# The one-tile up group of the second half of the MLP is worked between the two down groups of the first half

## The chip, the cores and the metric

The kernel runs on one NeuronCore of one Trainium2 chip. The metric is the device time of one execution in microseconds (us). Three executions of the kernel before took 1300.86, 1300.80 and 1301.01 us, a median of 1300.86.

## The reference, cut to what matters

One layer: a gated token mixer, then a convolutional gated MLP, then a last RMSNorm. Only the MLP is touched. There are 256 tokens, a width of 2048 and an inner width of 5504, which is 43 tiles of 128 features.

```
def conv_ffn(x, g_norm, w_up, conv_k, conv_b, w_down):
    h = rms_norm(x, g_norm)
    up = h @ w_up                                   # 2048 -> 2 * 5504: a gate and a value
    t = up.shape[1]
    pad = jnp.pad(up, ((0, 0), (1, 1), (0, 0)))
    up = (pad[:, :t] * conv_k[0] + pad[:, 1:t + 1] * conv_k[1]
          + pad[:, 2:t + 2] * conv_k[2] + conv_b)   # width 3 over the tokens
    gate, val = jnp.split(up, 2, axis=-1)
    return x + (jax.nn.silu(gate) * val) @ w_down   # 5504 -> 2048
```

All of it is float32.

## The kernel before

**Split numbers.** A float32 product is made of three products of float32r operands. Each weight piece is loaded into a raw slot (SP queue, L272), ScalarE writes its rounded high part (`high`, L316), and VectorE writes the low part, piece minus high part (`low`, L319). TensorE multiplies high by high, low by high and high by low (L483 to L485, or L459 and L467 where the weights are the stationary operand).

**Pieces and slots.** All weights lie in one stream of pieces, in the order in which `weight_stream` lists the groups. A usual piece is 512 KB (1024 columns by 128 rows, or two row tiles of 512 columns). There are five raw slots (`RAW`), each free again when high and low of its piece are made, and the load of the piece five places later waits for that. Six unit slots hold a high and a low part; a unit is free when TensorE has used it. At piece i the program prepares pieces up to i + 4 (`AHEAD`), then runs the small tasks that earlier steps have left for i, then issues TensorE's products. Each engine works its own list in order and waits on semaphores for the others.

**The MLP in two parts.** `FF_BLOCKS` cuts the 43 tiles into 22 and 21. Of each part the up groups come first, two feature tiles each (8 pieces of 512 KB, 4 PSUM banks); the second part has an odd number of tiles, so its first group, ("up", 22), has a single tile: 8 pieces of 256 KB and 2 banks. Behind an up group stand its evictions: `combine` (L854, L856) adds the two halves of the banks, `conv` (L1225 to L1233) scales and convolves, `gate` (L1238, L1240) makes silu(gate) times value, `split` (L1147, L1148) makes high and low of the result for the down groups. Then come two down groups, ("down", n, 0) and ("down", n, 1), for the left and the right 1024 output columns, one piece of 512 KB per feature tile.

**Pairs with seven products.** In a down group some pairs of pieces are worked with seven products where the plain way has eight (`FF_SEVEN`). For such a pair VectorE makes a half low and a full low (`plain`), then sums the two raw pieces in place (`summed`: L396, L400, L401; or L398 to L401 where the two raw slots don't adjoin), then makes two more full lows of the sums (`summed` and `last`). Only after these are the pair's two raw slots free. The second group of the first part has five such pairs, at its pieces 2, 6, 10, 14 and 18. `LATE_SUMS` names a pair whose sums are queued one step later. Some low parts are made early, stored in HBM and read back by the POOL queue (L350) in place of the subtraction: in this group those of pieces 1, 5 and 9.

**Banks.** A down group holds four banks for its plain products, and one each for the products 1, 5, 7 and 6 of its pairs: all eight. Behind the last pair `combine` of `wide_step` empties the extra four: `one` (L586, L591, L592) frees the banks of 1, 6 and 7, the first instruction of `both` (L586, on two rows) frees that of 5. At the end of the group two additions of 1024 columns (L1286) empty the other four. The next group takes the pairs of banks that were freed first.

Below, d0 to d21 are the pieces of ("down", 0, 1), u0 to u7 those of ("up", 22), and n0 to n7 those of ("up", 23), the first two-tile up group of the second part.

Of the kernel before, what the change touches and what calls it, by code (L numbers as in the profile page):

```python
# [18 lines left out]
KD = D // 128  # L19
# [4 lines left out]
DFF = 5504  # L24
# [17 lines left out]
RAW = 5  # L42
TB = 2
SUMS_LATE = 1
LATE_SUMS = ((("down", 0, 1), 2), (("down", 1, 1), 1))
ODD_AMONG = 1
UNITS = (4, 2)
WAKE = 20
# [22 lines left out]
def weight_stream():  # L71

    groups, order = {}, []

    def add(key, kind, w, pieces):
        groups[key] = (kind, w, pieces)
        order.extend([key] * len(pieces))

    def by_two(row0, nk, *blocks):
        return [([row0 + k for k in range(k0, min(k0 + 2, nk))], blocks) for k0 in range(0, nk, 2)]

    def nat(key, w, row0, nk, c0):
        add(key, "nat", w, by_two(row0, nk, (c0, 512)))

    def qk(j):
        add(("qk", j), "ws", "w_in", by_two(0, KD, (Q0 + j * 256, 256), (K0 + j * 256, 256)))

    def wide(key, w, c0, tiles):
        add(key, "wide", w, [([k], ((c0, 1024),)) for k in tiles])

    def branch(br, j):
        nat(("branch", br, j), "w_branch", br * 8, 8, j * 512)

    add(("vg",), "wide", "w_in", [([k], (("x", T), (V0, 1024))) for k in range(KD)])  # L100
    for j in range(2):
        add(("u", j), "ws", "w_in", by_two(0, KD, (U0 + j * 512, 512)))
    for j in range(2):
        nat(("va", j), "w_in", 0, KD, VA0 + j * 512)
        qk(j)
    for j in (2, 3):
        branch(0, 2 * j - 4)
        branch(0, 2 * j - 3)
        qk(j)
    for br in range(2):  # L110
        for c in range(2):
            wide(("gates", br, c), "w_in", (GA0, GB0)[br] + c * 1024, range(KD))
    for j in range(4):
        branch(1, j)
    for j in range(2):
        wide(("out", j), "w_out", j * 1024, range(KD))
    for n, (f0, f1) in enumerate(FF_BLOCKS):
        for f, nb in up_groups(n):
            add(("up", f), "ws", "w_up", by_two(0, KD, (f * 128, nb * 128), (DFF + f * 128, nb * 128)))
        for j in range(2):  # L120
            wide(("down", n, j), "w_down", j * 1024, down_tiles(n))
    return groups, order


def up_groups(n):

    f0, f1 = FF_BLOCKS[n]
    odd = (f1 - f0) % 2
    return [(f0, 1)] * odd + [(f, 2) for f in range(f0 + odd, f1, 2)]


def down_tiles(n):
    f0, f1 = FF_BLOCKS[n]
    return list(range(f0, f1))


def weight_pieces():

    groups, order = weight_stream()
    out, count, at = [], {}, 0  # L140
    for key in order:
        _, w, pieces = groups[key]
        tiles, blocks = pieces[count.get(key, 0)]
        count[key] = count.get(key, 0) + 1
        cols = sum(n for _, n in blocks)
        out.append((key, w, tiles, blocks, at, cols))
        at += 128 * len(tiles) * cols
    return out, at
# [19 lines left out]
def trunk_kernel(ctx, tc, x, weights, vectors, ln_g, ln_b, w_s_turned, b_s, rpb, norm_final, out):  # L168
# [59 lines left out]

    pieces, _ = weight_pieces()
    kinds = {key: g[0] for key, g in weight_stream()[0].items()}  # L230
    size_of = {key: len(g[2]) for key, g in weight_stream()[0].items()}
    starts = {}
    for i, p in enumerate(pieces):
# [138 lines left out]
    def sums(i):  # L372


        c0, c1 = slice(0, 512), slice(512, 1024)

        def plain():
            r0, r1 = raw[i][0], raw[i + 1][0]
            slot = half_free.pop(0)
            h, l = (slot[0].tile([128, 512], F32R, name=f"half_{p}{slot[1]}") for p in ("hi", "lo"))  # L380
            halves[i] = (h, l, slot)
            hb, lb = unit((i, "b"))
            high(h, r0[:, c0])
            high(hb, r1)
            low(l, r0[:, c0], h)
            if i + 1 in in_dram:
                nc.gpsimd.dma_start(lb, in_dram[i + 1])
            else:
                low(lb, r1, hb)

        def summed():
            (r0, (_, a)), (r1, (_, b)) = raw[i], raw[i + 1]
            ht, lt = unit((i, "t"))
            first = r0.rearrange("p (h c) -> p h c", h=2)
            if b == a + 1:
                nc.vector.tensor_add(first, first, raws[:, a:b + 1, c1])  # L396
            else:
                nc.vector.tensor_add(r0[:, c0], r0[:, c0], r0[:, c1])  # L398
                nc.vector.tensor_add(r0[:, c1], r0[:, c1], r1[:, c1])
            nc.vector.tensor_add(r1[:, c1], r1[:, c1], r0[:, c0])  # L400
            nc.vector.tensor_add(r1[:, c0], r1[:, c0], r1[:, c1])  # L401
            high(ht, r0)
            low(lt, r0, ht)
            raw_done(i)

        def last():
            r1 = raw[i + 1][0]
            h, l = unit((i, "s"))
            high(h, r1)
            low(l, r1, h)  # L410
            raw_done(i + 1)

        return plain, summed, last
# [4 lines left out]
    def plan():  # L418
        i = 0
        while i < len(pieces):  # L420
# [4 lines left out]
            if i in seven:  # L425
                plain, summed, last = sums(i)
                late = SUMS_LATE if (pieces[i][0], i - starts[pieces[i][0]]) in LATE_SUMS else 0
                queue.extend([(i, 1, 1, plain), (i + 1 + late, 1, 0, summed), (i + 1 + late, 1, 0, last)])
# [1126 lines left out]
```

## Time and profile before

| | |
|---|---|
| median of three runs | 1300.86 us |
| the profiled execution's own time | 1301.52 us |
| span of its trace (first to last instruction) | 1299.7 us |
| TensorE busy | 1289.3 us, 99% of the span |
| VectorE busy | 1048.7 us, 81% |
| ScalarE busy | 767.0 us, 59% |
| mean granted TensorE clock | 0.998 of full speed |
| moved by DMA | 285.02 MB, a mean of 219 GB/s |

The busy time of TensorE is modelled: a product of 512 columns is shown with 0.39 us, but the next one starts 0.227 us later. So the starts of its rows tell more than the busy share. "Idle before" a row, in brackets with what ended it, shows where an engine waited.

### The profile page before, as it was taken

The page shows a single profiled execution, that of the slowest core. Times are in us where ns is not written, and L with a number is a line of the kernel's source. Part 1 is how long each engine was busy: PE and PEld are TensorE (multiplying, and loading weights), DVE is VectorE, ACT ScalarE, POOL GpSimd, SP SyncE. Part 2 cuts the span into 40 slices and gives each one's busy share as a digit, 9 for nine tenths or more (in the row PEclk, how much of TensorE's full clock was granted, in tenths as well). Part 3 has the DMA queues.
Part 4 walks back from the last instruction along what each step waited for, and adds up shares of the span by engine and source line. Part 5 has one row for each costly group of instructions (what it writes and reads, how often), then busy time and mean ns, then how long its engine had stood idle before and what let it go on. Part 6 is the DMA issues. An engine that isn't in the chain of part 4 may idle for free.

```text
span 1299.7 us, 18682 instructions
## 1 busy us (share of the span) xinstructions
PE 1289.3 (99%) x6739; PEld 1102.4 (85%) x6739; DVE 1048.7 (81%) x1416; ACT 767.0 (59%) x1104; POOL 118.4 (9%) x235
## 2 busy tenths in 40 slices
PE   9999999999999999999999999999999999999997
PEld 7888888888888888888888888888888888888886
DVE  5686677877889878887888888898986878887887
ACT  5865566665655645565666556564655655565664
POOL 0502064530000000000000000000000000000000
PEclk9999999999999999999999999999999999999999
DMA  8966686555555656657667777677577676765873
GB/s 328 327 189 195 207 229 188 176 191 179 172 200 198 229 178 237 227 193 252 200 206 235 237 232 212 206 241 240 203 275 244 213 227 220 233 213 177 279 258 124
DMA packets 82685, 285.02 MB, mean 219 GB/s; under 512 B 10528, under 2 KB 11680, under 8 KB 82080
## 3 DMA queue, kind: packets, MB, share of 16 engines
q1 hardware_dynamic: 72144, 260.53, 61.1%
q0 software_dynamic: 10160, 23.03, 5.8%
q8 instruction: 53, 0.87, 0.3%
q14 instruction: 40, 0.33, 0.1%
q10 hardware_dynamic: 288, 0.27, 0.1%
HBM read 271.72 MB, written 9.96 MB: 217 GB/s over the span
## 4 chain that ended last, share of the span: by engine, by line
PE 95%; DMA 2%; DVE 2%; ACT 1%; issue 0%; SPq 0%; DVEq 0%; ACTq 0%
PE banks L459 31%; PE banks L467 16%; PE banks L483 15%; PE banks L484 15%; PE banks L485 15%; DMA start<-in_weights_dram 2%; DMA raws<-in_weights_dram 1%; PE banks L990 1%; DVE units L319 1%; PE banks L503 1%; PE banks L501 0%; PE banks L500 0%; PE banks L1042 0%; ACT units L316 0%; PE banks L864 0%; PE banks L1192 0%
## 5 line engine op out<-in xcount | busy, mean ns | idle before, releaser
L319 DVE TENSOR_TENSOR units<-raws,units 128x1024 fp32r<-128x1024 f32 (+1 forms) x470 | 560.8, 1213 | 112.7 <-ACT units L316 103.9
L316 ACT ACTIVATE units<-raws 128x1024 fp32r<-128x1024 f32 (+1 forms) x485 | 496.5, 1046 | 216.7 <-PE banks L484 53.1
L459 PE MATMUL banks<-h,units 128*128 128x512 f32 x1760 | 415.2, 391 | 0.0
L459 PEld LDWEIGHTS banks<-h,units 128*128 128x128 f32 x1760 | 324.9, 188 | 64.6
L467 PEld LDWEIGHTS banks<-h,units 128*128 128x128 f32 x1760 | 215.7, 188 | 5.8
L467 PE MATMUL banks<-h,units 128*128 128x256 f32 x1760 | 217.8, 279 | 0.0
L1228 ACT ACTIVATE tc<-ta,vec 128x256 f32<-128x256 f32 x86 | 47.1, 594 | 98.3 <-DVE ta L1225 98.3
L483 PE MATMUL banks<-units,h 128*128 128x512 f32 x266 | 104.5, 393 | 0.0
L485 PE MATMUL banks<-units,h 128*128 128x512 f32 x266 | 103.6, 390 | 0.0
L484 PE MATMUL banks<-units,h 128*128 128x512 f32 x266 | 103.5, 389 | 0.0
L856 DVE TENSOR_TENSOR ta<-banks,tb 128x512 f32<-128x512 f32 x55 | 35.5, 685 | 54.7 <-ACT tb L854 54.7
L484 PE MATMUL banks<-units,a 128*128 128x512 f32 (+1 forms) x196 | 75.4, 385 | 0.0
L483 PE MATMUL banks<-units,a 128*128 128x512 f32 (+1 forms) x196 | 75.4, 385 | 0.0
L485 PE MATMUL banks<-units,a 128*128 128x512 f32 (+1 forms) x196 | 75.4, 385 | 0.0
L854 ACT ACTIVATE tb<-banks 128x512 f32<-128x512 f32 x55 | 29.9, 595 | 76.5 <-PE banks L459 76.4
L1231 DVE SCALAR_TENSOR_TENSOR tc<-ta,vec,tc 128x255 f32<-128x255 f32 x86 | 41.4, 481 | 28.9 <-ACT tc L1228 28.9
L485 PEld LDWEIGHTS banks<-units,h 128*128 128x128 f32 x266 | 49.9, 188 | 10.6
L483 PEld LDWEIGHTS banks<-units,h 128*128 128x128 f32 x266 | 50.0, 188 | 10.1
L484 PEld LDWEIGHTS banks<-units,h 128*128 128x128 f32 x266 | 50.0, 188 | 9.9
L484 PE MATMUL banks<-units,s 128*128 128x512 f32 x148 | 57.6, 389 | 0.0
L485 PE MATMUL banks<-units,s 128*128 128x512 f32 x148 | 57.6, 389 | 0.0
L483 PE MATMUL banks<-units,s 128*128 128x512 f32 x148 | 57.6, 389 | 0.0
(253 smaller groups left out, 1688.8 us busy)
## 6 DMA issues: line engine op xcount, KB each, us to landing
raws<-in_weights_dram SPq DMA_DIRECT2D x461, 512.0 KB, 4.5
start<-in_weights_dram SPq DMA_DIRECT2D x13, 640.0 KB, 6.4
units<-low POOLq DMA_DIRECT2D x15, 512.0 KB, 6.1
low<-half_hi POOLq DMA_DIRECT2D x15, 256.0 KB, 6.3
low<-half_lo POOLq DMA_DIRECT2D x15, 256.0 KB, 7.2
xs<-in_x_dram SPq DMA_DIRECT2D x2, 1024.0 KB, 10.5
vw<-va POOLq DMA_DIRECT2D x32, 64.0 KB, 6.1
x<-in_x_dram POOLq DMA_DIRECT2D x2, 1024.0 KB, 7.0
```

The source lines that it names most:

```text
L316: nc.scalar.activation(h, w, AF.Copy)
L319: nc.vector.tensor_sub(l, w, h.bitcast(F32))
L459: nc.tensor.matmul(p, h[:, c:c + 128], acts(2 * n + k), start=n == 0 and k == 0, stop=n == last and k == tiles - 1)
L467: nc.tensor.matmul(p[:, :T], l[:, c:c + 128], acts(2 * n + k)[:, 0, :], start=False, stop=False)
L483: nc.tensor.matmul(p, xh, wh, start=start, stop=False)
L484: nc.tensor.matmul(p, xl, wh, start=False, stop=False)
L485: nc.tensor.matmul(p, xh, wl, start=False, stop=stop)
L503: nc.tensor.matmul(box["ps"][2 * b + c], acts(n, b)[0], l[:, cs], start=False, stop=last)
L854: nc.scalar.activation(t, p[:, :, T:], AF.Copy)
L856: nc.vector.tensor_add(a, p[:, :, :T], t)
L1228: nc.scalar.activation(v, u, AF.Identity, scale=ck[:, 1, ch:ch + 1], bias=ck[:, 3, ch:ch + 1])
L1231: nc.vector.scalar_tensor_tensor(v[:, 1:], u[:, :T - 1], ck[:, 0, ch:ch + 1], v[:, 1:], op0=OP.mult, op1=OP.add)
```

## The change

`weight_stream` lists the groups of the second part without its first, and lists that one between the two down groups of the first part. The order was: down 0 left, down 0 right, up 22, up 23, ... It is now: down 0 left, up 22, down 0 right, up 23, ... The pair at d2 and d3 is also taken out of `LATE_SUMS`, so its sums stand at their usual place.

```
-LATE_SUMS = ((("down", 0, 1), 2), (("down", 1, 1), 1))
+LATE_SUMS = ((("down", 1, 1), 1),)
...
+    def up(f, nb):
+        add(("up", f), "ws", "w_up", by_two(0, KD, (f * 128, nb * 128), (DFF + f * 128, nb * 128)))
...
     for n, (f0, f1) in enumerate(FF_BLOCKS):
-        for f, nb in up_groups(n):
-            add(("up", f), "ws", "w_up", by_two(0, KD, (f * 128, nb * 128), (DFF + f * 128, nb * 128)))
-        for j in range(2):
-            wide(("down", n, j), "w_down", j * 1024, down_tiles(n))
+        for f, nb in up_groups(n)[n:]:
+            up(f, nb)
+        wide(("down", n, 0), "w_down", 0, down_tiles(n))
+        if n == 0:
+            up(*up_groups(1)[0])
+        wide(("down", n, 1), "w_down", 1024, down_tiles(n))
```

No instruction is added or removed; the number of instructions of every engine stays as it was. In the changed file the lines of the MLP's code stand five further on (L319 is L324).

The first place is VectorE between the first pair (d2, d3) and the second (d6, d7). Before, from the first pair's last three full lows (d2/d3's sums and d4) on:

```order
L319 TENSOR_TENSOR units<-raws,units 128x1024 x3
L319 TENSOR_TENSOR half_lo_7558<-raws,half_hi_7557 128x512
L319 TENSOR_TENSOR units<-raws,units 128x1024
L396 TENSOR_TENSOR raws<-raws 128x1024
L400 TENSOR_TENSOR raws<-raws 128x512
L401 TENSOR_TENSOR raws<-raws 128x512
L319 TENSOR_TENSOR units<-raws,units 128x1024 x3
```

Now, from behind the first of the same three lows on (`ta`, `tb` and `tc` are the up group's eviction, `comb` its gated result):

```order
L861 TENSOR_TENSOR ta<-banks,tb 128x512
L324 TENSOR_TENSOR units<-raws,units 128x1024 x2
L1230 TENSOR_TENSOR ta<-ta,rb 128x512
L1236 SCALAR_TENSOR_TENSOR tc<-ta,vec,tc 128x255
L1238 SCALAR_TENSOR_TENSOR tc<-ta,vec,tc 128x255
L1236 SCALAR_TENSOR_TENSOR tc<-ta,vec,tc 128x255
L1238 SCALAR_TENSOR_TENSOR tc<-ta,vec,tc 128x255
L1245 TENSOR_TENSOR comb<-tc 128x2x128
L324 TENSOR_TENSOR half_lo_7661<-raws,half_hi_7660 128x512
L324 TENSOR_TENSOR units<-raws,units 128x1024
L403 TENSOR_TENSOR raws<-raws 128x512
L404 TENSOR_TENSOR raws<-raws 128x512
```

The eviction of the up group, which stood among the lows of the next up group, now stands between two pairs.

The second place is VectorE from the last pair's sums (d18, d19) to the additions that end the group. Before:

```order
L319 TENSOR_TENSOR units<-raws,units 128x1024 x4
L319 TENSOR_TENSOR units<-raws,units 128x512 x3
L586 TENSOR_TENSOR x_4371<-x_4371,comb 128x512
L591 TENSOR_TENSOR comb<-comb,banks 128x512
L592 TENSOR_TENSOR comb<-comb,banks 128x512
L586 TENSOR_TENSOR x_4371<-x_4371,banks 128x2x512
L586 TENSOR_TENSOR x_4371<-x_4371,comb 128x512
L586 TENSOR_TENSOR x_4371<-x_4371,comb 128x2x512
L319 TENSOR_TENSOR units<-raws,units 128x512
L1286 TENSOR_TENSOR x_4371<-banks,x_4371 128x1024 x2
```

Now:

```order
L324 TENSOR_TENSOR units<-raws,units 128x1024 x6
L324 TENSOR_TENSOR half_hi_7947<-raws,half_hi_7947 128x512
L324 TENSOR_TENSOR half_lo_7951<-raws,half_lo_7951 128x512
L324 TENSOR_TENSOR units<-raws,units 128x1024
L591 TENSOR_TENSOR x_4371<-x_4371,comb 128x512
L596 TENSOR_TENSOR comb<-comb,banks 128x512
L597 TENSOR_TENSOR comb<-comb,banks 128x512
L591 TENSOR_TENSOR x_4371<-x_4371,banks 128x2x512
L591 TENSOR_TENSOR x_4371<-x_4371,comb 128x512
L591 TENSOR_TENSOR x_4371<-x_4371,comb 128x2x512
L324 TENSOR_TENSOR units<-raws,units 128x1024
L1291 TENSOR_TENSOR x_4371<-banks,x_4371 128x1024 x2
```

Where three half-size lows (u0 to u2) stood ahead of the four instructions that free the extra banks, there are now three full ones (n0 to n2) and two halves of a low that is made early for a later group.

## Rows read from the trace of the kernel before

**Rows 1.** Waits of TensorE: total us, times, longest us (the only row).
```profile
PE banks L717 <- POOL ident masks.py:199: 1.4, 1, 1.4
```

**Rows 2.** Busy us by stage: second down group, up 22, last stretch.
```profile
core 0: us, PE busy (x) PEld busy (x) DVE busy (x) ACT busy (x) POOL busy (x), PEclk, DMA share, GB/s
...
893.95:950.60 56.65, 56.65 (x251) 46.92 (x250) 51.13 (x55) 30.60 (x35) 1.05 (x2) 1.00 0.58 195
950.60:961.60 11.00, 11.00 (x65) 9.69 (x65) 8.97 (x11) 5.15 (x7) 0.30 (x1) 1.00 0.72 261
...
1290.00:1299.70 9.70, 0.81 (x7) 0.61 (x6) 4.82 (x14) 2.89 (x9) 0.00 (x0) 0.78 0.58 216
```

**Rows 3.** Timeline of TensorE, single products: start us, us, line, names.
```profile
913.24 0.39 PE L485 MATMUL banks<-units,s 128*128 128x512 f32 x1
...
950.19 0.84 PE L459 MATMUL banks<-h,units 128*128 128x512 f32 x3
...
961.01 1.07 PE L459 MATMUL banks<-h,units 128*128 128x512 f32 x4
```

**Rows 4.** Timeline of VectorE from the first pair's sums to the second's.
```profile
899.78 3.65 DVE L319 TENSOR_TENSOR units<-raws,units 128x1024 fp32r<-128x1024 f32 x3
...
905.78 1.22 DVE L319 TENSOR_TENSOR units<-raws,units 128x1024 fp32r<-128x1024 f32 x1 [1.60 <-ACT units L316]
...
909.51 1.22 DVE L319 TENSOR_TENSOR units<-raws,units 128x1024 fp32r<-128x1024 f32 x1
```

**Rows 5.** Timeline of ScalarE: the high part that waits for a load.
```profile
904.68 1.06 ACT L316 ACTIVATE units<-raws 128x1024 fp32r<-128x1024 f32 x1 [1.23 <-DMA raws<-in_weights_dram]
```

**Rows 6.** Timeline of VectorE, ends of both down groups.
```profile
889.75 0.69 DVE L586 TENSOR_TENSOR x<-x,comb 128x512 f32<-128x512 f32 x1
...
894.92 2.35 DVE L1286 TENSOR_TENSOR x<-banks,x 128x1024 f32<-128x1024 f32 x2
...
938.49 5.99 DVE L319 TENSOR_TENSOR units<-raws,units 128x1024 fp32r<-128x1024 f32 x6
...
945.50 0.68 DVE L586 TENSOR_TENSOR x<-x,comb 128x512 f32<-128x512 f32 x1
...
947.61 1.21 DVE L586 TENSOR_TENSOR x<-x,banks 128x1024 f32<-128x1024 f32 x1
...
953.35 2.49 DVE L319 TENSOR_TENSOR units<-raws,units 128x512 fp32r<-128x512 f32 x4
```

**Rows 7.** DMA issues, KB, us to landing: SP at 901.02, 955.26; beside POOL 873.86, 886.70.
```profile
raws<-in_weights_dram SPq DMA_DIRECT2D x1, 512.0 KB, 3.6
...
raws<-in_weights_dram SPq DMA_DIRECT2D x1, 512.0 KB, 5.6
...
raws<-in_weights_dram SPq DMA_DIRECT2D x1, 512.0 KB, 6.8
...
raws<-in_weights_dram SPq DMA_DIRECT2D x1, 512.0 KB, 7.6
```

**Rows 8.** Timeline of VectorE: four full lows in a row, and the eviction of up 22.
```profile
928.89 4.79 DVE L319 TENSOR_TENSOR units<-raws,units 128x1024 fp32r<-128x1024 f32 x4
...
964.52 0.68 DVE L856 TENSOR_TENSOR ta<-banks,tb 128x512 f32<-128x512 f32 x1
...
967.39 0.68 DVE L1225 TENSOR_TENSOR ta<-ta,rb 128x512 f32<-128x512 f32 x1
...
970.58 1.22 DVE L319 TENSOR_TENSOR units<-raws,units 128x1024 fp32r<-128x1024 f32 x1
971.71 0.42 DVE L1240 TENSOR_TENSOR comb<-tc 128x256 f32<-128x256 f32 x1
```

**Rows 9.** DMA issue by SP at 922.81, third of its burst.
```profile
raws<-in_weights_dram SPq DMA_DIRECT2D x1, 512.0 KB, 5.1
```

**Rows 10.** Timeline and chain: TensorE's transposes near the start and at 557 us.
```profile
1.38 4.25 PE L717 MATMUL banks<-ident 128*128 128x128 f32 x20 [1.38 <-POOL ident masks.py:199]
...
557.01 0.87 PE banks L1192 x8
```

## The prediction

> **What bounds the kernel now.** I read four views in this order. First the waits by engine: of all its waits TensorE has one row, 1.4 us at the program's start [rows 1]. Then the busy table by stage: in the second down group and in up 22 TensorE is busy for all of each window at a granted clock of 1.00, while VectorE has 51.1 of 56.65 us [rows 2]. Then TensorE's timeline: from the first product of up 22 at 950.19 to that of up 23 at 961.2 lie 11.0 us [rows 3], which is 32 products of 512 columns at 0.227 us and 32 of 256 columns at 0.117, with nothing between them. So TensorE sets the time, and no wait of it is left to win. What the change can do is to bring a wait in. Last, then, VectorE's timeline, to see by how much it is ahead of TensorE.
>
> In the second down group it is little ahead. The low of a pair's second sum (d7) is made by 909.51 + 2.5 = 912.0 [rows 4], and TensorE's first product with it stands at 913.24 [rows 3]: 1.2 us of reserve. The pairs go round in a loop: from the first sum's low of one pair (899.78) to that of the next (909.51) takes 9.73 us [rows 4], where TensorE takes 45 products, 10.2 us. The loop is not VectorE's work alone: it idles 1.60 us in it [rows 4], because the pair's second raw piece is loaded only when that low has freed a slot, lands 3.6 us later [rows 7], is rounded by ScalarE [rows 5], and then come a low and the sums.
>
> **The change part by part.** The 64 products, 16 VectorE and 13 ScalarE instructions and 8 loads of up 22 stand 22 pieces earlier, on SP ahead of d0's load and on POOL ahead of the three reads of stored lows. Their count stays, and TensorE's total with it: 0 us. d0 to d21 move by 11.0 us, and up 23 is still due at 961.2. Whether it starts then is a question of three places.
>
> *The start of the second down group.* At the end of the first, `one` began at 889.75 and the last addition ended at 894.92 + 2.35 = 897.3 [rows 6]. Ahead of `one` stood a full low that waited for its high; now it is a half-size one, which I put 1.4 us earlier (0 to 1.5). One half-size low (u3) is new ahead of the additions, 0.6 us each by four in 2.49 [rows 6]: they end at 896.5. Then u4 to u7 free a raw slot every 0.6 us, for d1 at 897.1 and for d3 at 898.3. Such a third load of a burst took 5.6 us to land; beside a read by POOL others took 6.8 and 7.6 [rows 7], and POOL's read for d1 falls right here. So d3 lands at 903.9 to 905.9, at 901.9 if as quickly as a first one (3.6); I take 904.5, between 5.6 and 6.8. The Trainium skill (Trainium Kernel Development and Optimization, Key Constraints) says that transfers issued from the SP and POOL queues run on the same engines and interleave; by that it would be 6.8 and the result below 0.6 us more, without it 0.6 us less.
>
> From a pair's landed piece to its first sum's low are 909.51 - 904.68 = 4.83 us [rows 4, 5]: that low starts at 909.3. Before, moved by 11.0, it would be 910.8. So VectorE enters the group 1.5 us further ahead, which the light pieces and the earlier sums (`LATE_SUMS`) give.
>
> *Between the first pair and the second.* Now the eviction of up 22 stands here. VectorE does three full lows (3.65 [rows 4]), the addition of the banks (0.68), the convolution (967.39 to 970.58, 3.19, a wait for ScalarE included), the gating (0.42) [rows 8], a half low (0.6), a full low (1.2) and four sums of 0.69 (two raw slots that don't adjoin): 12.5 us where the loop took 9.73, with no load late any more. In the place that the eviction has left, among the lows of up 23, nothing was late, so nothing comes back there. The second pair's first low starts at 921.8, against 920.5 for the kernel before moved by 11.0. Its second sum's low is ready 1.2 + 0.4 (the split of the gated result) + 1.2 later, at 924.6; TensorE wants it at 913.24 + 11.0 = 924.2. That is a first wait of some 0.4 us.
>
> The three pairs that follow go by the loop, which the loads set: 938.49 - 909.51 = 29.0 us [rows 4, 6]. The last pair's first low starts at 950.8.
>
> *The end of the group.* Up 23 needs four banks where up 22 needed two: those of products 1, 6 and 7, which `one` frees, and that of 5, which the first instruction of `both` frees. Before, `one` stood behind half-size lows: from 938.49 to the end of `one` were 9.1 us and to the end of that instruction 10.3 [rows 6]. Now full ones stand there. Counted from the last pair's first low: four full lows 4.8 [rows 8]; n0 and n1 to 7.1; two halves of an early piece; n2, whose load waits for d20's slot (3.7), takes 5.1 to land as the third of its burst [rows 9], and 1.06 for its high, so that its low ends at 11.0; `one`, 945.50 to 947.61, 2.1 [rows 6], to 13.2; the first of `both`, 1.2, to 14.4. The banks are free at 964.0 and 965.2. TensorE wants the first at 961.2 and the last for its fourth product, 0.7 us later: it is 2.8 and 3.3 us late. If n2's load were hidden, n2 would end at 4.8 + 2.3 + 1.3 + 1.2 = 9.6, and 1.4 us less would be lost.
>
> Covered are: up 22's own banks (freed some 3 us ahead of its first product), the two that it hands on to products 7 and 6 of d3 (freed by 911.3; wanted 36 products of 0.227 us behind d0's start at 904.8, at 912.9), POOL's low of d1 (issued when TensorE is through u3's low, some 4 us into up 22, so by 897.9; landed by 905.5 with the 7.6 us of [rows 7]; wanted 14 products into the group, at 907.9), and the gated result, which only the second part reads. Each of these has over 1 us.
>
> **Sum.** The late 3.3 us is counted on the absolute clock, so the 0.4 us is in it. Behind up 23's start TensorE has no idle time in which to regain it. The span of the profiled execution goes from 1299.7 to 1303.0, its own time of 1301.52 to 1304.8. The median of the three runs shown lies 0.66 below that own time; on its footing 1300.86 + 3.3 = 1304.2 us.
>
> **Rivals.**
> *Hidden, or nearly.* TensorE wants the banks at 961.2, and each step has slack in it: with d3 landed at 901.9 and n2's load hidden the sum is 3.3 - 2.6 - 1.4, below zero, and the time stays 1300.9; with half of both it is 1302.2. For it speaks that VectorE enters the group ahead and that before every wait of TensorE is hidden; against it that the loop's length and the full lows ahead of `one` are counted from rows. This is the other side: not slower.
> *The clock falls.* A wait of some 3 us in one piece could cost the clock. In the last 9.7 us TensorE works for 0.81 us and then idles, and the mean granted clock of that window is 0.78 [rows 2], so it does fall when TensorE idles long enough. At the lower level (1.2 GHz) transposes start 4.25 / 20 = 0.21 us apart, at the higher (2.4 GHz) 0.87 / 8 = 0.11 [rows 10]; a stretch as long as that at the start, 4.25 us, would lose 2.1: 1306.3. Against it: the gap is split in two, and some products fall into its end (the first banks come 1.2 us before the last). The Trainium skill (TensorE: Matmul & The Clock Gate, Part 1) has the rule that an idle TensorE is throttled to half rate until it has been busy again; no wait in the middle of this trace shows it.
> *Faster.* In the kernel before no load is issued between 886.70 and 901.02 [rows 7] while the late sums hold the slots; that hole goes. But its price is paid out of VectorE's lead, and TensorE has only the 1.4 us at the start to give back: 1300.8.
>
> **How the numbers follow.** What a measurement of this kernel can tell from no change is 0.2%, 2.6 us: faster means under 1298.3, slower over 1303.5. The forecast, a wait of 2.6 to 5.5 us, gets 0.58; hidden or nearly 0.33; the fallen clock 0.06; faster 0.03. So slower 0.64, same 0.33, faster 0.03. The predicted time is that of the likeliest, 1304.2. The bounds of the unknown costs are 0 (above) and, with d3 at 905.9 and `one` no earlier than before, 3.3 + 1.4 + 1.4 = 6.1. The range runs from 1301.2, which leaves the wholly hidden case out, to 1306.2. The forecast's own range is 1303.5 to 1306.2.
>
> **What the profile after would show.** Right: TensorE's waits name VectorE's L597 or L591 with 2.5 to 5 us at the start of up 23 and at most 1.5 us at d7 or d8; from the first pair's to the second's first low some 12.5 us, and 9.7 between later ones; `one` ends some 13 us behind the last pair's first low. Wrong: TensorE's only row is again the one at the start (the lead sufficed), or the wait stands at d0 to d3 (the loads or the banks of up 22 are late), or rows behind up 23's start run at half the clock. A gap much larger than 5 us would mean that the loop had been lengthened too.

## The result, and the profile after

The changed kernel takes 1308.63 us (median of four, 1307.68 to 1310.12) where the kernel before takes 1300.93 beside it: a ratio of 1.0058, 95% interval [1.0046, 1.0069]. It is slower, as forecast, but by 7.7 us and not by 3.3, and the time lies above the range. The profiled execution has a span of 1307.0 us, 7.3 more than before.

TensorE's waits after the change (us in total, times, longest), where before there was one row [rows 1]:

```profile
PE banks L464 <- DVE comb L597: 3.6, 1, 3.6
PE banks L722 <- POOL ident masks.py:199: 1.4, 1, 1.4
PE banks L490 <- DVE units L324: 1.1, 2, 0.7
PE banks L488 <- ACT units L321: 0.4, 1, 0.4
PE banks L472 <- DVE units L324: 0.2, 1, 0.2
```

The first row is the start of up 23, which waits for `one`; that of L488 and 0.7 of L490's 1.1 are the second pair; the 0.2 of L472 stands at 80.75 us, far ahead of the change. The lines of the functions behind the first edit are five higher than before (L597 was L592).

VectorE's timeline: the first sum's low of the five pairs of the second down group, then the end of `one` and the first instruction of `both` (start us, us). They answer to [rows 4, 6]:

```profile
910.75 1.22 DVE L324 TENSOR_TENSOR units<-raws,units 128x1024 fp32r<-128x1024 f32 x1
...
923.05 1.22 DVE L324 TENSOR_TENSOR units<-raws,units 128x1024 fp32r<-128x1024 f32 x1
...
933.48 4.79 DVE L324 TENSOR_TENSOR units<-raws,units 128x1024 fp32r<-128x1024 f32 x4
...
943.22 4.78 DVE L324 TENSOR_TENSOR units<-raws,units 128x1024 fp32r<-128x1024 f32 x4
...
953.05 1.22 DVE L324 TENSOR_TENSOR units<-raws,units 128x1024 fp32r<-128x1024 f32 x1
...
965.97 0.69 DVE L597 TENSOR_TENSOR comb<-comb,banks 128x512 f32<-128x512 f32 x1
966.57 1.21 DVE L591 TENSOR_TENSOR x<-x,banks 128x1024 f32<-128x1024 f32 x1
```

The distances are 12.30, 10.43, 9.74 and 9.83 us, and from the last low to the end of `one` 13.61. TensorE's timeline shows what came of it: up 23 starts at 966.80 where it was due at 961.2.

```profile
966.80 5.48 PE L464 MATMUL banks<-h,units 128*128 128x512 f32 x16 [3.62 <-DVE comb L597]
```

Its first 16 products take 5.48 us. With no wait ahead of them they take 3.80 (below, the run with the banks sooner). The busy table of the wait and of what follows it (PEclk is the third column from the end) tells why:

```profile
962.79:966.80 4.01, 0.39 (x3) 0.03 (x1) 3.35 (x5) 3.56 (x5) 0.18 (x1) 1.00 1.06 380
966.80:970.20 3.40, 3.40 (x8) 2.62 (x9) 3.40 (x4) 0.54 (x1) 0.00 (x0) 0.52 0.77 289
970.20:974.00 3.80, 3.80 (x26) 3.42 (x25) 3.80 (x5) 2.12 (x2) 0.00 (x0) 0.98 0.40 138
```

After the wait the granted clock is 0.52: eight products start 0.427 us apart, not 0.227, which is 1.6 us. The rule of the Trainium skill (TensorE: Matmul & The Clock Gate, Part 1), that an idle TensorE is throttled to half rate until it has been busy again, is here in the middle of the trace, where the kernel before had no wait to show it.

So TensorE loses 1.8 us at the second pair and 3.8 at up 23 (counted from start to start of the products, less their usual distance), 1.6 to the clock, and 0.6 at the first pair of ("down", 1, 0), whose wait is the rest of L490's row: 7.8. Its last product starts at 1298.41 against 1290.53, 7.9 later; the stretch behind it is 0.6 shorter, which gives the 7.3 of the span.

### The profile page after: what moved, and what is told of

It reads as the page before. It is cut to its first block, busy times and chain, and to the rows that moved or that the text cites. A ratio compares the mean times of both kernels' runs of the same rounds, so it can differ in the third digit from the quotient of the medians.

```text
span 1307.0 us, 18685 instructions
## 1 busy us (share of the span) xinstructions
PE 1291.9 (99%) x6739; PEld 1102.7 (84%) x6739; DVE 1047.9 (80%) x1416; ACT 766.8 (59%) x1104; POOL 119.2 (9%) x235
## 4 chain that ended last, share of the span: by engine, by line
PE 84%; DVE 6%; DMA 6%; ACT 2%; issue 1%; DVEq 0%; SPq 0%; ACTq 0%
PE banks L464 29%; PE banks L472 15%; PE banks L488 13%; PE banks L490 13%; PE banks L489 13%; DMA raws<-in_weights_dram 4%; DVE units L324 2%; DMA start<-in_weights_dram 2%; ACT units L321 1%; PE banks L995 1%; DVE raws L401 1%; DVE raws L405 0%; PE banks L1047 0%; DVE x L591 0%; PE banks L1197 0%
## 5 line engine op out<-in xcount | busy, mean ns | idle before, releaser
L324 DVE TENSOR_TENSOR units<-raws,units 128x1024 fp32r<-128x1024 f32 (+1 forms) x470 | 560.9, 1214 | 117.0 <-ACT units L321 105.2
L472 PEld LDWEIGHTS banks<-h,units 128*128 128x128 f32 x1760 | 215.7, 188 | 6.3 <-DVE units L324 0.4
L472 PE MATMUL banks<-h,units 128*128 128x256 f32 x1760 | 217.8, 279 | 0.2 <-DVE units L324 0.2
L488 PE MATMUL banks<-units,h 128*128 128x512 f32 x266 | 104.5, 393 | 0.0
L490 PE MATMUL banks<-units,h 128*128 128x512 f32 x266 | 103.6, 390 | 0.0
L488 PE MATMUL banks<-units,a 128*128 128x512 f32 (+1 forms) x196 | 75.4, 385 | 0.0
L490 PE MATMUL banks<-units,a 128*128 128x512 f32 (+1 forms) x196 | 75.4, 385 | 0.0
L490 PE MATMUL banks<-units,s 128*128 128x512 f32 x148 | 58.0, 392 | 1.1 <-DVE units L324 1.1
L490 PEld LDWEIGHTS banks<-units,h 128*128 128x128 f32 x266 | 49.9, 188 | 10.6
L488 PEld LDWEIGHTS banks<-units,h 128*128 128x128 f32 x266 | 50.0, 188 | 10.1
L488 PE MATMUL banks<-units,s 128*128 128x512 f32 x148 | 57.7, 390 | 0.4 <-ACT units L321 0.4
```

What stands on the lines that cost most here:

```text
L324: nc.vector.tensor_sub(l, w, h.bitcast(F32))
L472: nc.tensor.matmul(p[:, :T], l[:, c:c + 128], acts(2 * n + k)[:, 0, :], start=False, stop=False)
L488: nc.tensor.matmul(p, xh, wh, start=start, stop=False)
L490: nc.tensor.matmul(p, xh, wl, start=False, stop=stop)
```

## The experiments

My theory was that VectorE, not TensorE, sets the second down group after the move, by three costs: the load of d3, which sets the first pair; the eviction between the pairs; and the place of `one` and `both` behind full-size lows. The half rate would come of the wait. Each run undoes one of these. The kernel before ran beside each.

### The stored low of d1 left out

```
+    for made in early.values():
+        made[:] = [i for i in made if i != starts["down", 0, 1] + 1]
```

> The low half of d1 is no longer made ahead of time and read back by GpSimd; VectorE makes it as for other pieces. Load theory: the raw loads of d2, d3 and d4 landed 7.80, 8.02 and 8.81 us after their issue because GpSimd's read of 7.26 us shares the DMA engines with them; without it d3 lands some 1.4 us sooner after its issue (about 6.6 us), the first low of the first pair starts at 909.3 to 909.6 instead of 910.75, and the time falls by about 1.4 us, to 1307.2. VectorE's extra 1.2 us is hidden, since it was idle for 4.59 us ahead of 905.23. Rival, the burst of raw loads alone: the landings stay within 0.4 us, the first low at 910.4 or later, and the time stays at 1308.3 to 1309. In both the wait at the start of up 23 stays above 2 us.

Measured: 1306.46 us, ratio 1.0042 [1.0027, 1.0057]. The two DMA issues of the changed kernel, SP's at 897.80 (d3) and POOL's at 897.65, then the queues between that issue and its landing (packets, MB, share of 16 engines):

```profile
raws<-in_weights_dram SPq DMA_DIRECT2D x1, 512.0 KB, 8.0
...
units<-low POOLq DMA_DIRECT2D x1, 512.0 KB, 7.3
...
q1 hardware_dynamic: 564, 2.08, 73.6%
q0 software_dynamic: 144, 0.52, 22.6%
```

The same of this run (issue of d3 at 897.49), and VectorE's low that it leads to:

```profile
raws<-in_weights_dram SPq DMA_DIRECT2D x1, 512.0 KB, 6.5
...
q1 hardware_dynamic: 542, 1.97, 88.8%
```

```profile
909.10 1.22 DVE L324 TENSOR_TENSOR units<-raws,units 128x1024 fp32r<-128x1024 f32 x1
```

POOL's queue holds 22.6% of the DMA engines for 8.02 us, that is 1.8 us of them; without it the load lands in 6.5. Over the seven profiles of this study with the stored low d3 took 6.9 to 8.3 us, 7.6 in the mean, over the three without it 6.4 to 6.9, 6.6 in the mean. The Trainium skill (Trainium Kernel Development and Optimization, Key Constraints) states that the two queues share the engines. The shares agree with it: 96.2% for both together, of which the loads' queue has 73.6%, where it has 88.8% alone. The landing came out as the load theory had it, the first low 0.2 us sooner still, and the wait at up 23 stayed (3.0 us). The time fell by some 2 us where 1.4 was expected, though the two intervals overlap.

### The eviction of up 22 put off

```
-            at(i + 1, lambda: conv(0))
+            at(i + (23 if f0 == FF_BLOCKS[1][0] else 1), lambda: conv(0))
```

> Up 22 stands where the change puts it, but its convolution, gate and split (VectorE 0.68 + 4 x 0.48 + 0.43 + 0.42 us) run as late as before the change, in the second piece of up 23. Eviction theory: the second pair's first low comes 2.6 us sooner after the first pair's (9.7 instead of 12.30 us), the 1.8 us that TensorE lost at the second pair are gone, up 23 starts 2.6 us sooner with a wait of about 3.0 us, and the time is 1306.0 (1304.4 if the half-rate products go as well). Rival, loads set the distance of the pairs: it stays near 12 us and the time within 0.5 us of 1308.6.

Measured: 1304.23 us, ratio 1.0022 [1.0012, 1.0032]. VectorE's first lows of the first two pairs, and the start of up 23:

```profile
909.86 1.22 DVE L324 TENSOR_TENSOR units<-raws,units 128x1024 fp32r<-128x1024 f32 x1
...
919.45 3.66 DVE L324 TENSOR_TENSOR units<-raws,units 128x1024 fp32r<-128x1024 f32 x3
...
962.91 4.31 PE L464 MATMUL banks<-h,units 128*128 128x512 f32 x16 [1.79 <-DVE comb L597]
```

The distance is 9.59 us, so it is the eviction and not the loads that stretched it. The wait at the second pair is gone. Up 23 waits 1.8 us and not the 3.0 expected, mostly since d3 landed 0.9 us sooner in this execution (it took 7.2 us); the products behind that wait run at full clock (1.00 to 967). The median is that of the expected case in which the half-rate products go as well (1304.4).

### The banks emptied sooner

```
+                if key == ("down", 0, 1) and n < 2:
+                    at_once(i + 1, f)
+                    continue
```

> The change as it is, with the two steps that empty the banks of products 1, 6, 7 and 5 of the second down group placed ahead of the stored piece's halves and of the low of n2, and nothing else moved. Order theory: VectorE frees the first banks at about 962.4 and product 5's at 963.7, the wait of 3.6 us on L597 shrinks to 0.5 us or less, and with it go the eight products at half rate if the wait is what lowered the clock: 1303.2 (clock with the wait) or 1304.8 (clock for another reason). The 1.8 us at the second pair stay. Rival, up 23 waits for its first weights: the wait only changes its name to a low of units, and the time stays within 0.7 us of 1308.6.

Measured: 1302.81 us, ratio 1.0012 [1.0003, 1.0021]. The end of `one`, and up 23's first products:

```profile
961.85 0.69 DVE L597 TENSOR_TENSOR comb<-comb,banks 128x512 f32<-128x512 f32 x1
...
964.21 3.80 PE L464 MATMUL banks<-h,units 128*128 128x512 f32 x16
```

TensorE's waits, beside 1.4 us at the start:

```profile
PE banks L490 <- DVE units L324: 0.7, 1, 0.7
PE banks L488 <- ACT units L321: 0.4, 1, 0.4
```

The first banks are free at 962.5, where 962.4 was expected. The row of L597 is gone, and so is the half rate, while 1.1 us of waits at the second pair stay. The wait at up 23 is one of order and not of weights, and with the clock that it lowers it is most of the loss.

### The second edit undone, and done alone

The entry kept in the changed kernel:

```
-LATE_SUMS = ((("down", 1, 1), 1),)
+LATE_SUMS = ((("down", 0, 1), 2), (("down", 1, 1), 1))
```

> The change without its second edit: the entry for the pair at d2 stays in LATE_SUMS, so up 22's own bank is emptied ahead of that pair's sums. Theory that only the move counts: the first low of the first pair stays within 0.7 us of 910.75 and the time within 0.8 us of 1308.6. Rival, the entry decides how late the first pair is: the first low moves by more than 1.5 us and the time with it, to 1307.0 or below, or 1310.2 or above.

Measured: 1308.13 us, ratio 1.0058 [1.0042, 1.0074]. The first pair's first low stands at 910.78, the wait at up 23 is 2.9 us, and about eight products run at half rate. With the move the entry changes nothing that can be told. Then the same two lines the other way round in the kernel before, where up 22 stays in its place:

> The kernel before with only the entry for the pair at d2 taken out of LATE_SUMS; up 22 stays where it was. If the move carries the whole price: no wait of TensorE other than the first 1.4 us and the time within 0.4 us of before. If the entry costs on its own: a wait at the banks of the first down group's last sums (L1286 is one step later) and 0.5 us or more.

Measured: 1303.60 us, ratio 1.0019 [1.0010, 1.0028]. This I had wrong: of the two cases it is the second, and the entry costs 2.45 us on its own. TensorE's waits in that run:

```profile
PE banks L483 <- DVE x L1286: 1.9, 1, 1.9
PE banks L717 <- POOL ident masks.py:199: 1.4, 1, 1.4
PE banks L485 <- DVE units L319: 0.4, 1, 0.4
```

The sums and two lows then stand ahead of the additions that empty the first group's last banks (they start at 899.78, before at 894.92 [rows 6]), and d2 waits for them. With up 22 in between, d2 comes 11 us later, and this wait is gone. So the second edit costs nothing only beside the first, the first does not need the second, and none of the 7.7 us is the entry's.

### Cures together

Eviction put off and banks sooner, the edits as above:

> The change with both cures: up 22's convolution, gate and split as late as before the change, and the banks of products 1, 6, 7 and 5 emptied ahead of the stored piece's halves and of the low of n2. If the eviction between the pairs and the order at the group's end are the whole price: no wait at the second pair and none above 0.3 us at up 23, no products at half rate, time within 0.5 us of before. If the move costs something else as well (a longer way through the banks, transfers that collide later): still 1 us or more above before.

Measured: 1301.56 us, ratio 1.0001 [0.9992, 1.0010]. TensorE's only row is again that at the start:

```profile
PE banks L725 <- POOL ident masks.py:199: 1.4, 1, 1.4
```

With these two undone, then, nothing of the price is left that can be told. The two do not simply add up, since each of them shortens the lateness at up 23. Stored low left out and banks sooner:

> The change without the stored low of d1 and with the banks emptied sooner; up 22's eviction stays between the pairs. The two cures add up: the wait at the second pair is 0.2 to 0.6 us in place of 1.8, none at up 23, 0.3 to 0.8 us above before. If the landing of the loads was only chance in the run without the stored low: the wait at the second pair stays at 1.2 to 1.8 us and the time 1.3 us or more above before, like that of the run with the banks alone.

Measured: 1302.23 us, ratio 1.0009 [1.0000, 1.0018]: half a miss, 1.1 us above before where 0.3 to 0.8 was expected. At the second pair nothing of note is left, but in the profile the third pair waits 1.2 us, because the load that its sums wait for took 6.0 us (next part). All three:

> All three cures together. Each left-over wait of the stage is gone already with two of them, so the time is that of the run with the later eviction and the sooner banks within 0.3 us, and no lower than before by more than 0.3 us, since TensorE cannot start earlier than its products follow each other. If the early loads still cost with two cures: 0.4 to 1.0 us below that run.

Measured: 1300.69 us, ratio 0.9999 [0.9990, 1.0008]. That is 0.87 us below the run with the first two cures, where at most 0.3 was expected and 0.4 to 1.0 was to mean that the early loads still cost. The two intervals overlap, so whether they do stays open. No version is faster than the kernel before.

### The loop of 10.43 us

One term was still open: the loop behind the second pair, 10.43 us where the others take 9.7 to 9.8. Its load, issued at 924.30, took 4.3 us, and all seven other variants of the changed kernel so far had 4.3 to 6.0 for this one. Queues between its issue and landing, and its landing, in the changed kernel:

```profile
q1 hardware_dynamic: 212, 0.80, 63.9%
q8 instruction: 1, 0.02, 1.7%
...
raws<-in_weights_dram SPq DMA_DIRECT2D x1, 512.0 KB, 4.3
```

and in the run above with the load of 6.0:

```profile
q1 hardware_dynamic: 300, 1.10, 61.4%
q8 instruction: 1, 0.02, 2.7%
...
raws<-in_weights_dram SPq DMA_DIRECT2D x1, 512.0 KB, 6.0
```

One packet of instructions holds one engine for 1.7% of 16 x 4.33 us, which is 1.2 us, and for 2.6 us in the other run. The view does not tell the 16 engines apart, so how one engine held makes the whole load late is not shown. The matching load of the kernel before (issued at 910.75) has no such packet inside and took 3.5:

```profile
raws<-in_weights_dram SPq DMA_DIRECT2D x1, 512.0 KB, 3.5
```

To move the packet I changed only the number of transposes at the start of the changed kernel, which nothing reads:

```
-WAKE = 20
+WAKE = 32
```

> The changed kernel with 12 more transposes at the very start (32 for 20), which do no work for the result. In the profile after, a 16 KB packet of the instruction queue lies on a DMA engine from 925.3 to 926.5, inside the load that the second pair's loop waits for (issued 924.30, landed after 4.33 us where before the change it took 3.5). The packets of that queue come about every 27 us, as often as TensorE uses up a fixed number of instructions; 24 more of them at the start bring this packet some 2.7 us sooner in the program, ahead of that load's issue. If the packet delays the load: it lands in 3.4 to 3.8 us and the loop is 9.6 to 9.8 us in place of 10.43. If it does not: 4.2 us or more and 10.3 or more again. The start itself costs up to 2.4 us, so the time says nothing here.

and the same line with `WAKE = 2`:

> The changed kernel with 18 transposes fewer at the very start (2 for 20): 36 instructions of TensorE fewer ahead of the packet of the instruction queue, which then falls some 4 us later in the program, behind the landing of the load that the second pair's loop waits for. If the packet delays the load: it lands in 3.4 to 3.8 us and that loop is 9.6 to 9.8 us. If it does not: 4.2 us or more and 10.3 or more again. TensorE starts its first products at the lower clock, so the time says nothing here.

With 32, the queues and the landing of the load issued at 924.59, then VectorE's two first lows of the loop:

```profile
q1 hardware_dynamic: 167, 0.62, 63.3%
...
raws<-in_weights_dram SPq DMA_DIRECT2D x1, 512.0 KB, 3.6
```

```profile
923.35 1.22 DVE L324 TENSOR_TENSOR units<-raws,units 128x1024 fp32r<-128x1024 f32 x1
...
933.02 4.79 DVE L324 TENSOR_TENSOR units<-raws,units 128x1024 fp32r<-128x1024 f32 x4
```

With 2, the same of the load issued at 923.09, and the two lows:

```profile
q1 hardware_dynamic: 158, 0.58, 57.7%
...
raws<-in_weights_dram SPq DMA_DIRECT2D x1, 512.0 KB, 3.4
```

```profile
921.85 1.22 DVE L324 TENSOR_TENSOR units<-raws,units 128x1024 fp32r<-128x1024 f32 x1
...
931.30 4.79 DVE L324 TENSOR_TENSOR units<-raws,units 128x1024 fp32r<-128x1024 f32 x4
```

No row of instructions is left inside the load in either, and the loops are 9.67 and 9.45 us. With the packet moved either way the load is back at its usual time, so the packet was the delay. (Single runs: 1308.30 and 1304.87 us; with the start changed, they say nothing of the loop's price.)

## Why the prediction was wrong

The mechanism held in each part: TensorE waits for L597 at up 23 and a little at the second pair, and the eviction and the order at the group's end are what has to be undone. The sum failed in three sizes, and two costs that it put at nothing came on top.

- **The start of the second group.** The step "d3 lands at 904.5, between 5.6 and 6.8" was mis-sized. The load was issued at 897.80 (forecast 898.3) and took 8.02 us (I took 6.2), longer than the two loads beside POOL in [rows 7], 6.8 and 7.6. It landed at 905.82, just inside my own bound of 905.9. First low 910.75, not 909.3: +1.45. With it the lead of 1.5 us went that I had put down to the light pieces and the earlier sums: 910.75 is the kernel before moved by 11.0. What came sooner at VectorE waited there for the load.
- **Between the pairs.** 12.30 for 12.5 forecast: -0.2. Right, and shown by putting the eviction off. The first wait was 1.8 us and not 0.4, since VectorE came to it 1.25 us later than forecast.
- **The three loops.** "By the loop, which the loads set": 30.0 for 29.0, +1.0. Some 0.7 of it is the instruction packet in one load, which no row that I had picked showed.
- **The end of the group.** 13.61 for 13.2: +0.4. Right in kind; the run with the banks sooner shows that the place in VectorE's list decides.
- **Sum so far.** 964.0 + 1.45 - 0.2 + 1.0 + 0.4 = 966.65, where `one` ended at 966.66. On the clock of the forecast that is a start 5.6 us late.
- **The clock.** The rival I gave 0.06 took place, beside the forecast and not in its stead; its price, 2.1 us, was near the 1.6 measured. The argument against it (a gap split in two) did not hold: 3.8 us came in one piece. The forecast's further 0.5 us for the bank of 5 did not come either: that bank is free at 966.57 + 1.21 = 967.78, and the fourth product, slowed by the clock, starts only at 968.1.
- **No idle time behind up 23.** Half right: there was none to regain the loss in, but 0.6 us more was lost at ("down", 1, 0). Its first pair waits 0.2 to 0.6 us in six of the other runs too, the kernel before without the entry among them, so it can come without the move. The kernel before does not have it, and what sets it was not tried.

The range had its error in the same place: its upper bound put d3's load and the `one` of the first group at their worst, yet left the loop as it was and the clock out. It also stopped at 1306.2 where that bound of 6.1 us gives 1300.86 + 6.1 = 1306.96, without a reason; the measured 1308.63 lies above both.

## What to carry to other kernels

A group that is moved takes its evictions and its bank count with it: read, on the engine that frees banks, what stands ahead of the freeing step in its list, and place that step by when the banks are wanted. Where TensorE never waits before a change, price a first wait with the clock behind it, and the loads of a burst by their longest neighbours, with all that runs on the other queues. Two edits made together are best priced apart as well, since one may hide what the other alone would cost.

## What the runs showed of the hardware

- **Half rate behind a wait.** Waits of 1.95, 2.09 and 2.51 us (start to start, less the usual distance) left the clock at full; 2.62, 3.08, 3.12 and 3.79 were followed by seven to nine products at half rate. The two in the middle are 0.1 us apart, so the length of the wait alone may not be what decides; that stays open. A profile shows one execution: of the ten runs with the eviction put off, the three of 1305.4 to 1305.6 us have a mean granted clock of 0.997 and the seven of 1301.4 to 1304.5 us one of 0.998, so the half rate may come in some executions of one kernel and not in others. Busy tables of the products behind the waits of 2.62 (32 transposes) and 2.51 (2 transposes):

```profile
965.77:969.00 3.23, 3.19 (x8) 2.26 (x9) 3.23 (x4) 0.72 (x1) 0.00 (x0) 0.61 0.91 337
```

```profile
964.15:967.50 3.35, 3.24 (x13) 2.38 (x14) 3.35 (x4) 1.16 (x2) 0.00 (x0) 1.00 0.78 290
```

- **Instruction packets in the way of loads.** In the eight runs above a packet of 16 KB on the instruction queue held one DMA engine for 0.9 to 2.6 us, and the load of 512 KB under way with it landed 0.8 to 2.5 us later than the 3.5 without. In this stretch they come 27 to 29 us apart, and 24 instructions more or 36 fewer on TensorE at the program's start moved this one off the load. Not every packet delays: in the changed kernel the load issued at 893.27 has one inside, begun at 896.4 when most of the load was through, and landed in its usual time. Its rows:

```profile
q8 instruction: 1, 0.02, 1.7%
...
raws<-in_weights_dram SPq DMA_DIRECT2D x1, 512.0 KB, 3.6
```
